# First projection of a hybrid decoder step: eight weight blocks loaded beside the first token tile, three token buffers, layer-norm rows in borrowed buffers

## Chip, cores and metric

One NeuronCore of a Trainium2 chip runs the whole program. The metric is device time in microseconds (us) of one execution; lower is better. The runs of the kernel before gave 1758.77 us (median of 3, from 1756.23 to 1762.34).

## What is computed

The reference is one layer of a decoder trunk on 1088 tokens (1024 of a prompt, 64 of eight samples). Only its first steps matter here:

```python
xp = layer_norm(x_prompt, ln_emb_g, ln_emb_b)        # 1024 tokens x 1024
xs = layer_norm(x_sample, ln_emb_g, ln_emb_b)        # 64 tokens x 1024
...
(a_b, a_c, a_h, g_q, g_k, g_v, g_gate, g_a, g_b, n_q, n_kv, n_win, n_gate) = split_in(x @ w_in)
...
def layer_norm(x, g, b):
    mu = jnp.mean(xf, axis=-1, keepdims=True)
    var = jnp.mean(jnp.square(xf - mu), axis=-1, keepdims=True)
    y = (xf - mu) * lax.rsqrt(var + LN_EPS) * g + b
```

Matmuls are made nearly exact by splitting both operands into a rounded high part and the rest, and adding three products (high x high, high x low, low x high).

## The kernel before

The program has four stages: phase_a (layer norm of the nine token tiles and the input projections, then the delta rule's preparation), attention woven with the delta rule and the samples' branch, the output projection, and the feed-forward stage. All loads and stores are issued by SP (SyncE), in one queue. The instructions of each engine are put in order by a scheduler when the program is built: it moves instructions past each other by its own estimate of when they can start, but on the chip each engine then follows its order strictly, and an instruction that waits holds up all behind it.

The change lies in the first part of phase_a (lines 271 to 354). It computes the 800 columns of w_in that belong to the keys, values, window rows and gates, by token tiles: nat = LN(x) @ w_in[:, those columns].

- **Weights.** Eight blocks of 128 rows x 792 columns (396 KB each, tile nraw, L302) are split into nh (rounded copy, ScalarE, L310) and nl (the rest, VectorE, L311; GpSimd for blocks 5 and 7, by SPP). Their raw buffers are four (NRAW). The eight remaining columns come as graw (two loads with runs of 16 bytes, L307).
- **Token tiles.** load_x(t) brings tile t (128 x 1024, 512 KB) into one of five buffers xt (L286). norm(t) (L290) normalises it in place, stores it to x0_d (L293; read again by a later stage) and transposes it with eight TensorE transposes into PSUM tiles tpx, from which ScalarE writes x0h (L173) and VectorE x0l (L175). The transposes share two PSUM buffers of tag tp with the setup transposes pcw and pst (L1835, L1850).
- **Layer norm** (L116 to L130): VectorE statistics (bn_stats, L121), GpSimd power for the inverse root (rs, L127), VectorE (x - mean) * gB (L128), ScalarE scaling by rs (L129), and the addition of bB, by VectorE for tiles 0 and 1 and by GpSimd from tile 2 on (LNV = 2, L130). gB and bB hold the two layer-norm rows on all 128 partitions; each comes as a 512 KB load that reads the same row 128 times (L297, L298).
- **Products.** rows(t) (L317) runs 48 matmuls pn of 400 columns for tile t (two halves of 24); tile 8 (the samples) has 32. The loop at L345 loads tile t+3, normalises tile t, and runs rows(t-1).

After it come the blocks of the delta rule (pjg), whose weights wra are loaded by load_w into the two buffers of pool wr (tag "wr") and split into wha and wla in pool wp (tags "wh" and "wl").

## Time and profile before

| | |
|---|---|
| median of the runs shown | 1758.77 us (1756.23 to 1762.34) |
| the profiled execution | 1755.33 us |
| its span, first to last instruction | 1753.6 us |
| PE (TensorE) busy | 1651.2 us, 94% |
| DVE (VectorE) | 901.8 us, 51% |
| ACT (ScalarE) | 654.8 us, 37% |
| POOL (GpSimd) | 607.0 us, 35% |
| granted TensorE clock, mean | 0.973 |

The span is read by stages. A stage in which PE is busy throughout is bound by its instructions; one with idle time is bound by what PE waits for there. The granted clock is given as a share of full speed: 1.00 is 2.4 GHz, 0.50 is 1.2 GHz.

### The profile page before, as it was taken

The page shows a single profiled execution, that of the slowest core. Times are in us where ns is not written, and L with a number is a line of the kernel's source. Part 1 is how long each engine was busy: PE and PEld are TensorE (multiplying, and loading weights), DVE is VectorE, ACT ScalarE, POOL GpSimd, SP SyncE. Part 2 cuts the span into 40 slices and gives each one's busy share as a digit, 9 for nine tenths or more (in the row PEclk, how much of TensorE's full clock was granted, in tenths as well). Part 3 has the DMA queues.
Part 4 walks back from the last instruction along what each step waited for, and adds up shares of the span by engine and source line. Part 5 has one row for each costly group of instructions (what it writes and reads, how often), then busy time and mean ns, then how long its engine had stood idle before and what let it go on. Part 6 is the DMA issues. An engine that isn't in the chain of part 4 may idle for free.

```text
span 1753.6 us, 26082 instructions
## 1 busy us (share of the span) xinstructions
PE 1651.2 (94%) x9683; PEld 1501.8 (86%) x9683; DVE 901.8 (51%) x2339; ACT 654.8 (37%) x1392; POOL 607.0 (35%) x514
## 2 busy tenths in 40 slices
PE   5999999998989999988799999999999999999995
PEld 4999999986867877776678999999999999999994
DVE  6444666466776678786765333332342323423237
ACT  4324552123575656565654312212222122221233
POOL 5322461222264323243544422323224132241326
PEclk9999999999698999999899999999999999999998
DMA  9622246536165454413132211112111111120102
GB/s 314 231 63 61 85 156 139 156 106 164 43 141 114 121 157 131 146 58 106 54 122 68 73 37 37 49 38 60 37 46 52 35 49 40 45 61 25 49 15 104
DMA packets 192492, 157.33 MB, mean 90 GB/s; under 512 B 60236, under 2 KB 165742, under 8 KB 192238
## 3 DMA queue, kind: packets, MB, share of 16 engines
q1 hardware_dynamic: 192366, 155.67, 30.1%
q8 instruction: 76, 1.25, 0.3%
q14 instruction: 50, 0.41, 0.1%
HBM read 116.72 MB, written 43.04 MB: 91 GB/s over the span
## 4 chain that ended last, share of the span: by engine, by line
PE 78%; DVE 8%; DMA 5%; ACT 3%; POOL 2%; issue 2%; SPq 2%; DVEq 0%; ACTq 0%; POOLq 0%
PE puv L207 5%; PE puv L205 5%; PE puv L206 5%; PE pug L205 5%; PE pug L206 5%; PE pug L207 5%; PE pd L206 4%; PE pd L205 4%; PE pd L207 4%; PE pas L1130 2%; PE pat L1189 2%; PE pao L1204 1%; PE pjg L207 1%; PE pjg L206 1%; PE pjg L205 1%
## 5 line engine op out<-in xcount | busy, mean ns | idle before, releaser
L197 POOL TENSOR_TENSOR wlf<-wrf,whf 128x1024 fp32r<-128x1024 f32 x44 | 105.5, 2398 | 318.7 <-ACT whf L196 296.3
L1792 DVE TENSOR_TENSOR acc<-acc,pd 128x512 f32<-128x512 f32 x146 | 99.4, 686 | 198.2 <-PE pd L207 162.4
L207 PE MATMUL puv<-x1l,whf 128*128 128x384 f32 (+1 forms) x528 | 173.1, 328 | 0.0
L205 PE MATMUL puv<-x1h,whf 128*128 128x384 f32 (+1 forms) x528 | 173.0, 328 | 0.0
L206 PE MATMUL puv<-x1h,wlf 128*128 128x384 f32 (+1 forms) x528 | 172.9, 328 | 0.0
L205 PE MATMUL pug<-x1h,whf 128*128 128x384 f32 (+1 forms) x528 | 172.8, 327 | 0.0
L206 PE MATMUL pug<-x1h,wlf 128*128 128x384 f32 (+1 forms) x528 | 172.4, 326 | 0.0
L207 PE MATMUL pug<-x1l,whf 128*128 128x384 f32 (+1 forms) x528 | 172.3, 326 | 0.0
L1748 ACT COPY fg<-pug 128x384 f32<-128x384 f32 (+1 forms) x88 | 31.9, 389 | 344.6 <-PE pug L207 344.6
L205 PE MATMUL pd<-dh,hs 128*128 128x512 f32 x352 | 138.1, 392 | 2.8 <-DVE acc L1790 2.5
L206 PE MATMUL pd<-dh,hs 128*128 128x512 f32 x352 | 138.0, 392 | 0.0
L207 PE MATMUL pd<-dl,hs 128*128 128x512 f32 x352 | 138.0, 392 | 0.0
L1165 POOL TENSOR_TENSOR ass<-ass,az 128x256 f32<-128x256 f32 (+6 forms) x56 | 71.7, 1299 | 165.6 <-DVE az L1159 91.3
L1769 POOL TENSOR_TENSOR dl<-wdr,dh 128x1024 fp32r<-128x1024 f32 x22 | 52.7, 2398 | 180.0 <-ACT dh L1768 180.0
L1130 PE MATMUL pas<-K,aq 128*128 128x320 f32 (+5 forms) x384 | 103.6, 372 | 8.8 <-DVE amx L1137 7.6
L233 DVE SCALAR_TENSOR_TENSOR fz<-fg,w_f,fz 128x1024 f32<-128x1024 f32 x88 | 88.8, 1061 | 28.3 <-ACT fz L231 28.3
L206 PEld LDWEIGHTS puv<-x1h,wlf 128*128 128x128 f32 x528 | 99.8, 189 | 2.1
L206 PEld LDWEIGHTS pug<-x1h,wlf 128*128 128x128 f32 x528 | 99.3, 188 | 2.0
L205 PEld LDWEIGHTS puv<-x1h,whf 128*128 128x128 f32 x528 | 99.8, 189 | 1.3
L207 PEld LDWEIGHTS pug<-x1l,whf 128*128 128x128 f32 x528 | 99.1, 188 | 1.8
L205 PEld LDWEIGHTS pug<-x1h,whf 128*128 128x128 f32 x528 | 99.2, 188 | 1.6 <-ACT x1h L173 0.2
L207 PEld LDWEIGHTS puv<-x1l,whf 128*128 128x128 f32 x528 | 99.7, 189 | 1.1
(586 smaller groups left out, 4277.2 us busy)
## 6 DMA issues: line engine op xcount, KB each, us to landing
wrf<-in_w_up_dram SPq DMA_DIRECT2D x44, 512.0 KB
wdr<-in_w_down_dram SPq DMA_DIRECT2D x22, 512.0 KB
aq<-q_d SPq DMA_DIRECT2D x32, 256.0 KB
wra<-in_w_in_dram SPq DMA_DIRECT2D x14, 512.0 KB
xt<-in_x_prompt_dram SPq DMA_DIRECT2D x8, 512.0 KB
x_d<-xt SPq DMA_DIRECT2D x8, 512.0 KB
sv_d<-gsv SPq DMA_DIRECT2D x8, 512.0 KB
ma_d<-gma SPq DMA_DIRECT2D x8, 512.0 KB
```

The costliest lines, as they stand in the source:

```text
L197: c.nc.gpsimd.tensor_tensor(lo, raw, hi, op=OP.subtract)
L205: c.nc.tensor.matmul(out, ah(k), bh(k), start=start and j == 0, stop=False)
L206: c.nc.tensor.matmul(out, al(k), bh(k), start=False, stop=False)
L207: c.nc.tensor.matmul(out, ah(k), bl(k), start=False, stop=stop and j == n - 1)
L233: nc.vector.scalar_tensor_tensor(o, src(i), wcol(i), o, op0=OP.mult, op1=OP.add)
L1130: nc.tensor.matmul(p[:, :step], u.q[:, h, 4 * kv + g0 + g], c.K[:, kk, ks], start=h == 0, stop=h == 1)
L1165: nc.gpsimd.tensor_tensor(x[:, g, :n], x[:, g, :n], z[:, b, g:g + 1].to_broadcast([128, n]), op=OP.mult)
L1189: nc.tensor.transpose(pt[:, a, g], (SW if b else SS)[:, g, t * 128:t * 128 + 128], c.ident)
L1204: nc.tensor.matmul(po, v, tl[:, a], start=False, stop=j + a == len(steps) - 1)
L1748: nc.scalar.copy(dst, b3(p[:, o:o + m]) if three else p[:, o:o + m])
L1769: nc.gpsimd.tensor_tensor(dl, raw, dh, op=OP.subtract)
L1792: nc.vector.tensor_tensor(a, a, p, op=OP.add)
```

## The change

1. The eight weight blocks are loaded in a row, right behind tile 0, before graw and the other token tiles. Six have a buffer each in their own pool; blocks 6 and 7 use one "wh" and one "wl" buffer of the delta rule's weights.
2. gB and bB live in the two "wr" buffers. Of each, SP loads one partition (4 KB); TensorE multiplies it by a row of ones (two matmuls of 512 columns each, plain f32), and ScalarE copies the products over gB and bB, on all partitions.
3. Token tiles have three buffers, not five, and the loop loads two ahead, not three.
4. All nl subtractions and all additions of bB are VectorE's.

```diff
-            wnr = e1.enter_context(tc.tile_pool(name="wr", bufs=NRAW, reuse_waits="tile"))
+            wnr = e1.enter_context(tc.tile_pool(name="wr", bufs=6, reuse_waits="tile"))
...
-            gB = wn.tile([128, D], F32, name="gB")
-            bB = wn.tile([128, D], F32, name="bB")
+            gB = wr.tile([128, D], F32, name="gB", tag="wr")
+            bB = wr.tile([128, D], F32, name="bB", tag="wr")
...
-                xts[t] = ld.tile([128, D], F32, name="xt", bufs=5)
+                xts[t] = ld.tile([128, D], F32, name="xt", bufs=3)
...
-                layer_norm(c, xts[t], r, gB, bB, xts[t], small, "0", nc.vector if t < LNV else nc.gpsimd)
+                layer_norm(c, xts[t], r, gB, bB, xts[t], small, "0", nc.vector)
...
             load_x(0)
-            nc.sync.dma_start(gB, bcast(I["ln_emb_g"], D))
-            nc.sync.dma_start(bB, bcast(I["ln_emb_b"], D))
+            for x, y in ((gB, "ln_emb_g"), (bB, "ln_emb_b")):
+                nc.sync.dma_start(x[0:1], bcast(I[y], D, 1))
             raws8 = []
             for k in range(KD):
-                raw = wnr.tile([128, 792], F32, name="nraw")
-                held = nc.sync.dma_start(raw, w_in[k * 128:(k + 1) * 128, 2312:3104])
+                pool, tag = ((wnr, "nraw"), (wp, "wh"), (wp, "wl"))[max(k - 5, 0)]
+                raw = pool.tile([128, 792 if k < 6 else 1024], F32, name="nraw", tag=tag)[:, 0:792]
+                nc.sync.dma_start(raw, w_in[k * 128:(k + 1) * 128, 2312:3104])
                 raws8.append(raw)
-                if k == 1:
-                    graw = wn.tile([128, KD, 8], F32, name="graw")
-                    for j, s in enumerate((1796, 1792)):
-                        nc.sync.dma_start(graw[:, :, 4 * j:4 * j + 4], w_in[:, s:s + 4].rearrange("(k p) n -> p k n", p=128))
-                if k == 0:
-                    norm(0)
-                nc.scalar.copy(nh[:, k, 0:792], raw)
-                (nc.gpsimd if k in SPP else nc.vector).tensor_tensor(nl[:, k, 0:792], raw, nh[:, k, 0:792], op=OP.subtract)
+            graw = wn.tile([128, KD, 8], F32, name="graw")
+            for j, s in enumerate((1796, 1792)):
+                nc.sync.dma_start(graw[:, :, 4 * j:4 * j + 4], w_in[:, s:s + 4].rearrange("(k p) n -> p k n", p=128))
+            load_x(1)
+            one = wn.tile([1, 128], F32, name="one")
+            nc.vector.memset(one, 1.0)
+            for x in (gB, bB):
+                for h in range(2):
+                    p = c.ps.tile([128, 512], F32, name="pgB", tag="mm", bufs=c.nb["mm"])
+                    nc.tensor.matmul(p, one, x[0:1, 512 * h:512 * h + 512], start=True, stop=True)
+                    nc.scalar.copy(x[:, 512 * h:512 * h + 512], p)
+            norm(0)
+            for k in range(KD):
+                nc.scalar.copy(nh[:, k, 0:792], raws8[k])
+                nc.vector.tensor_tensor(nl[:, k, 0:792], raws8[k], nh[:, k, 0:792], op=OP.subtract)
...
-            load_x(1)
-            load_x(2)
...
-                if t + 3 < NT:
-                    load_x(t + 3)
+                if t + 2 < NT:
+                    load_x(t + 2)
```

What the scheduler makes of it, at three places. A row is an instruction: line, operation, output <- inputs, shape; x3 stands for three in a row. In the changed file the lines of the layer norm and of transpose_split are 2 smaller, those of setup 4 larger.

**VectorE, from the first statistics on.** xt_112 is token tile 0, xt_135 tile 1, xt_199 tile 2 of the changed program; nraw are the weight blocks in their order. Before:

```order
L121 BN_STATS st0_118<-xt_112 128x6 x2
L123 BN_AGGR mv0_121<-st0_118 128x2
L125 TENSOR_SCALAR ve0_123<-mv0_121 128x1
L128 SCALAR_TENSOR_TENSOR xt_112<-xt_112,mv0_121,gB_107 128x1024
L130 TENSOR_TENSOR xt_112<-xt_112,bB_108 128x1024
L311 TENSOR_TENSOR nl_110<-nraw_116,nh_109 128x792
L311 TENSOR_TENSOR nl_110<-nraw_147,nh_109 128x792
L313 TENSOR_TENSOR nl_110<-graw_149,nh_109 128x8x8
L175 TENSOR_TENSOR x0l_86<-tpx0_131,x0h_85 128x4x128
```

And with the change, behind the same three rows:

```order
L317 TENSOR_TENSOR nl_110<-nraw_120,nh_109 128x792
L126 SCALAR_TENSOR_TENSOR xt_112<-xt_112,mv0_154,gB_107 128x1024
L317 TENSOR_TENSOR nl_110<-nraw_122,nh_109 128x792
L317 TENSOR_TENSOR nl_110<-nraw_124,nh_109 128x792
L317 TENSOR_TENSOR nl_110<-nraw_126,nh_109 128x792
L128 TENSOR_TENSOR xt_112<-xt_112,bB_108 128x1024
L317 TENSOR_TENSOR nl_110<-nraw_128,nh_109 128x792
L317 TENSOR_TENSOR nl_110<-nraw_130,nh_109 128x792
L319 TENSOR_TENSOR nl_110<-graw_132,nh_109 128x8x8
L119 BN_STATS st0_203<-xt_135 128x6 x2
L173 TENSOR_TENSOR x0l_86<-tpx0_164,x0h_85 128x4x128
L119 BN_STATS st0_288<-xt_199 128x6 x2
```

All eight blocks now stand ahead of tile 0's x0l (two blocks stand ahead of the first row shown), and the statistics of tile 1 do too; before, only two blocks and graw did.

**SP's queue after tile 2's load (changed program).** out_5 are the eight copies of the samples' old window rows from DRAM to DRAM, cw and strow the setup loads, xt_201, xt_286 and xt_371 tiles 3, 4 and 5.

```order
L286 DMA xt_199<-in_x_prompt_dram 128x1024
L1835 DMA cw_381<-in_conv_a_w_dram 6x128
...
L1744 DMA out_5_dram<-in_cache_nsa_win_dram 16x8064 x3
L291 DMA x0_d_63<-xt_112 128x1024
L1744 DMA out_5_dram<-in_cache_nsa_win_dram 16x8064 x5
L286 DMA xt_201<-in_x_prompt_dram 128x1024
L291 DMA x0_d_63<-xt_135 128x1024
L291 DMA x0_d_63<-xt_199 128x1024
L337 DMA kw_d_66<-nat_230 128x768
L339 DMA out_2_dram<-nat_230 128x512
L286 DMA xt_286<-in_x_prompt_dram 128x1024
L286 DMA xt_371<-in_x_prompt_dram 128x1024
```

Before, tiles 1 to 4 were loaded ahead of the out_5 copies, and only tile 5 stood behind seven of them. Now tiles 3 and on stand behind all eight.

**TensorE, from the end of tile 2's products to the beginning of tile 3's (changed program).** pn_496 is the second half of tile 2, tpx0_455 and tpx0_462 are tile 3's transposes, tpx0_540 the first of tile 4's, pn_555 and pn_581 tile 3's two halves.

```order
L205 MATMUL pn_496<-nl_110,x0h_85 128x400
L1854 MATMUL pst_420<-ident_74,strow_418 128x88
L1854 MATMUL pst_426<-ident_74,strow_424 128x88
L1854 MATMUL pst_432<-ident_74,strow_430 128x88
L1854 MATMUL pst_438<-ident_74,strow_436 128x88
L169 MATMUL tpx0_455<-ident_74,xt_201 128x128 x4
L169 MATMUL tpx0_462<-ident_74,xt_201 128x128 x4
L203 MATMUL pn_555<-nh_109,x0h_85 128x400
L203 MATMUL pn_581<-nh_109,x0h_85 128x400
L169 MATMUL tpx0_540<-ident_74,xt_286 128x128 x4
```

On VectorE the copies out of those pst tiles stand behind tile 5's layer norm (the rows between the last two copies are memsets of later masks and are not shown):

```order
L126 SCALAR_TENSOR_TENSOR xt_371<-xt_371,mv0_615,gB_107 128x1024
L1856 COPY st_g_377<-pst_404 128x3x6 x7
L1856 COPY st_g_377<-pst_415 128x3x6
L128 TENSOR_TENSOR xt_286<-xt_286,bB_108 128x1024
L128 TENSOR_TENSOR xt_371<-xt_371,bB_108 128x1024
L1856 COPY st_f_378<-pst_420 128x2x22 x2
L1856 COPY st_f_378<-pst_426 128x2x22 x2
L336 COPY gab_105<-nat_469 128x32
L1856 COPY st_f_378<-pst_432 128x2x22 x2
L1856 COPY st_f_378<-pst_438 128x2x22 x2
...
L173 TENSOR_TENSOR x0l_86<-tpx0_455,x0h_85 128x4x128
```

Before, the setup transposes were spread over the middle of tiles 1 and 2, with 24 matmuls between one pair and the next; now four of them stand in a row at the boundary of tiles 2 and 3. From the tile products on, TensorE's order is the same in both programs until the attention stage has begun, differs there (about 1,500 rows in which neighbours change places), and is the same again from the output projection's end on.

## Rows read from the trace of the kernel before

**Rows 1.** The page: the span, each engine's busy time, and the chain that ended last, by engine.
```profile
span 1753.6 us, 26082 instructions
...
PE 1651.2 (94%) x9683; PEld 1501.8 (86%) x9683; DVE 901.8 (51%) x2339; ACT 654.8 (37%) x1392; POOL 607.0 (35%) x514
...
PE 78%; DVE 8%; DMA 5%; ACT 3%; POOL 2%; issue 2%; SPq 2%; DVEq 0%; ACTq 0%; POOLq 0%
```
**Rows 2.** Busy time by stage: stretch (us), its length, busy us of PE, PEld (weight loads), DVE, ACT, POOL with instructions, granted clock, DMA share, GB/s.
```profile
0.00:40.30 40.30, 20.16 (x96) 17.61 (x96) 28.07 (x57) 18.89 (x24) 18.59 (x17) 0.92 0.94 312
40.30:109.66 69.36, 69.36 (x400) 68.40 (x401) 25.06 (x58) 18.25 (x33) 21.67 (x14) 1.00 0.50 188
109.66:400.00 290.34, 283.93 (x1759) 268.69 (x1759) 172.10 (x448) 107.83 (x216) 98.57 (x119) 1.00 0.40 111
400.00:910.00 510.00, 455.21 (x2940) 380.25 (x2939) 366.52 (x1237) 289.90 (x768) 195.28 (x184) 0.93 0.41 113
910.00:1753.60 843.60, 822.51 (x4494) 766.88 (x4492) 310.08 (x542) 219.96 (x353) 272.88 (x181) 0.99 0.16 50
```
**Rows 3.** The chain of waits at the first part: start, us, what. One row for the eight transposes ahead of the products of tiles 4 to 7.
```profile
65.48 0.87 PE tpx L171 x8
...
75.12 0.87 PE tpx L171 x8
...
84.74 0.87 PE tpx L171 x8
...
94.37 0.64 PE tpx L171 x8
```
**Rows 4.** TensorE in order of time: start, us, instruction, [idle before <- releaser]: its start, its wait in tile 0, two matmuls of tile 8 that follow each other, and the first of the delta rule's blocks.
```profile
11.08 1.94 PE L171 MATMUL tpx<-ident,xt 128*128 128x128 f32 x8 [11.08 <-DVE xt L130]
...
23.94 0.70 PE L205 MATMUL pn<-nh,x0h 128*128 128x400 f32 x1 [5.78 <-ACT nh L310]
...
108.93 0.35 PE L214 MATMUL pn<-nh,x 128*128 128x400 f32 x1
109.11 0.35 PE L215 MATMUL pn<-nl,x 128*128 128x400 f32 x1
...
109.66 0.34 PE L205 MATMUL pjg<-x0h,wha 128*128 128x384 f32 x1
```
**Rows 5.** SP's issues of weight blocks 4 to 7, with start and us.
```profile
18.60 0.36 SPq L302 DMA_DIRECT2D nraw<-in_w_in_dram  x1
...
20.48 0.33 SPq L302 DMA_DIRECT2D nraw<-in_w_in_dram  x1
...
22.12 0.35 SPq L302 DMA_DIRECT2D nraw<-in_w_in_dram  x1
...
23.52 0.52 SPq L302 DMA_DIRECT2D nraw<-in_w_in_dram  x1
```
**Rows 6.** The first 60 us, by tile: operation, count, shortest/median/longest ns, first and last start, shapes: first the instructions on xt, then those on nraw, then x0l.
```profile
L121 DVE BATCH_NORM_STATS2 st<-xt x12: 643/680/695, 4.4 to 44.1; 128x6 f32<-128x512 f32 x12
L128 DVE SCALAR_TENSOR_TENSOR xt<-xt,mv,gB x6: 1277/1281/2833, 7.1 to 47.0; 128x1024 f32<-128x1024 f32 x6
L129 ACT ACTIVATE xt<-xt,rs x6: 1147/1150/1152, 8.5 to 48.7; 128x1024 f32<-128x1024 f32 x6
L130 DVE TENSOR_TENSOR xt<-xt,bB x2: 1175/1200/1225, 9.7 to 23.9; 128x1024 f32<-128x1024 f32 x2
...
L310 ACT CAST nh<-nraw x8: 834/852/860, 9.6 to 31.6; 128x792 fp32r<-128x792 f32 x8
L311 DVE TENSOR_TENSOR nl<-nraw,nh x6: 973/978/985, 10.9 to 30.0; 128x792 fp32r<-128x792 f32 x6
...
L175 DVE TENSOR_TENSOR x0l<-tpx,x0h x9: 677/692/692, 12.8 to 56.9; 128x512 fp32r<-128x512 f32 x9
```
**Rows 7.** VectorE's first wait for a load, and ScalarE's copy of a product out of PSUM (the nearest row to the copies of gB and bB).
```profile
4.42 1.28 DVE L121 BATCH_NORM_STATS2 st<-xt 128x6 f32<-128x512 f32 x2 [2.84 <-DMA xt<-in_x_prompt_dram]
...
45.99 0.49 ACT L326 COPY nat<-pn 128x400 f32<-128x400 f32 x1 [3.92 <-PE pn L207]
```
**Rows 8.** The columns of rows 2, over the first loads: gB and bB until about 6, then weight blocks, graw from about 9, weight blocks and token tiles from 11.
```profile
3.50:6.00 2.50, 0.00 (x0) 0.00 (x0) 1.51 (x4) 0.00 (x0) 0.00 (x0) 1.00 1.02 261
6.00:8.50 2.50, 0.00 (x0) 0.00 (x0) 1.42 (x2) 0.00 (x0) 0.55 (x1) 1.00 1.01 400
8.50:11.00 2.50, 0.00 (x0) 0.00 (x0) 1.29 (x2) 2.39 (x3) 0.00 (x0) 1.00 0.85 140
14.00:18.00 4.00, 4.00 (x22) 3.82 (x21) 4.00 (x6) 1.16 (x2) 0.00 (x0) 1.00 0.97 376
```
**Rows 9.** TensorE, two plain f32 matmuls of 512 columns that follow each other, and what such a group's instructions take each.
```profile
207.79 1.02 PE L661 MATMUL pgg<-gZ,gkT 128*128 128x512 f32 x2
...
L661 PE MATMUL pgg<-gZ,gkT x32: 590/592/595, 206.8 to 276.2; 128*128 128x512 f32 x32
```
**Rows 10.** The columns of rows 2, around the first idle time of TensorE: the granted clock is the third figure from the end.
```profile
0.00:11.00 11.00, 0.00 (x0) 0.00 (x0) 4.86 (x10) 3.89 (x5) 1.24 (x7) 1.00 0.80 223
11.00:18.00 7.00, 6.92 (x32) 6.33 (x32) 6.57 (x10) 3.18 (x6) 0.00 (x0) 1.00 0.98 361
18.00:21.00 3.00, 0.16 (x1) 0.00 (x0) 3.00 (x8) 0.00 (x0) 0.73 (x1) 1.00 1.01 359
21.50:24.00 2.50, 0.06 (x1) 0.06 (x1) 2.50 (x7) 2.00 (x2) 1.51 (x2) 0.50 0.87 273
24.00:27.50 3.50, 3.35 (x12) 2.79 (x12) 3.50 (x7) 2.45 (x3) 1.82 (x2) 0.50 0.94 273
28.00:28.50 0.50, 0.16 (x1) 0.16 (x2) 0.50 (x1) 0.29 (x1) 0.50 (x1) 1.00 1.10 374
```
**Rows 11.** SP's issue of the out_5 copies and of tile 5 behind them, and VectorE's wait for that tile.
```profile
25.47 5.63 SPq L1740 DMA_DIRECT2D out_dram<-in_cache_nsa_win_dram  x7
31.59 0.35 SPq L288 DMA_DIRECT2D xt<-in_x_prompt_dram  x1
...
43.49 1.29 DVE L121 BATCH_NORM_STATS2 st<-xt 128x6 f32<-128x512 f32 x2 [0.85 <-DMA xt<-in_x_prompt_dram]
```
**Rows 12.** A pair of setup transposes and the copies out of one of them.
```profile
45.79 0.32 PE L1850 MATMUL pst<-ident,strow 88*128 88x88 f32 x2
...
46.07 0.54 DVE L1852 COPY st_f<-pst 128x44 f32<-128x44 f32 x4 [1.29 <-PE pst L1850]
```

More of the change, by code (lines that the diff above doesn't have):

```diff
@@ L46 @@
 NRAW = 4
-LNV = 2
 ENDS = 2
@@ L50 @@
 GSV = 3
-SPP = (5,7)
 ORDER = (0, 1, 2, 3, 4, 5, 6, 7)
```

## The prediction

> **What bounds the kernel now.** First the page: PE is busy for 1651.2 of 1753.6 us, and the chain that ended last lies on PE for 78% [rows 1]. So only PE's idle time can be won, and the next view is busy time by stage [rows 2]: PE lacks 20.1 us in the first 40.3 us, nothing from there to 109.66, 54.8 us in the attention stretch (400 to 910), and little elsewhere. The change works on the first stretch.
>
> How much is lost there is worked out from its end. From 40.3 to 109.66 PE is never idle [rows 2], and a tile recurs every 9.63 us [rows 3]: 0.87 for eight transposes and 48 matmuls at 0.182, the distance of two that follow each other [rows 4], 8.76. Eight tiles are 77.0 us, tile 8 is 32 x 0.182 + 0.64 = 6.5, the eight setup transposes about 1.2 (pairs of 0.32 [rows 12]): 84.7 us. The delta rule's first block begins at 109.66 [rows 4], so the stage runs as if PE had begun at **25.0** and never waited. Where the 25 us go: PE first works at 11.08, then waits in tile 0 for nh of weight block 4 until 23.94 [rows 4]. Blocks 4 to 7 are issued only from 18.6 on, when the four raw buffers come free [rows 5]. Meanwhile the clock has fallen to half and comes back at about 28 [rows 10].
>
> **The change, part by part. Loads.** Tile 0 is seen at 4.42 [rows 7]. Before, gB and bB (1 MB) followed; now two single rows do, so the weight blocks move ahead of 1 MB. Eight blocks of 0.406 MB at the 400 GB/s of the stretch from 6 to 8.5 [rows 8] are 1.01 us each. At that rate tile 0's bytes are through near 3.75, and I keep a lag of 0.7 to 1.0 from last byte to use, as tile 0 shows. Blocks are seen at 5.6, 6.6 and so on to 12.7. graw's short runs cost about 2.5 us at 140 GB/s [rows 8] wherever they stand; behind the blocks they end near 14.4, and tiles 1 and 2 (0.52 MB each at 376 GB/s [rows 8]) are seen at about 17 and 18.
>
> The Trainium skill, "DMA: Bandwidth & Descriptors", section Specifications, gives some 358 GB/s as what HBM yields to one core. The stretch at 400 GB/s speaks against taking it here; by it the blocks would come every 1.13 us, tile 1 at nearly 18, and the gain below would be about 2.1 instead of 2.5.
>
> **The rows of the layer norm.** Four f32 matmuls of 512 columns, each two passes at a distance of 1.02 - 0.59 = 0.43 us [rows 9]: 3.5 us, in which PE has nothing else to do. Four copies out of PSUM at some 0.5 (0.49 for 400 columns [rows 7]) stand between ScalarE's weight copies. ScalarE's stream from 5.6 on is 8 x 0.85 + 4 x 0.5 + 1.15 [rows 6], about 10 us: its last nh ends near 15.5. The single-row load has no row; I take 0.5 us behind tile 0, and up to 2 us more is covered, since the copy of gB's second half stands behind three weight copies (until 8.7).
>
> **Tile 0.** VectorE's order now decides. By its durations [rows 6] and ScalarE's stream: blocks 0 to 2 until 9.8, (x - mean) * gB until 11.1, blocks 3 to 5 until 14.3 (block 5 waits for nh, which waits for the scaling of tile 0), + bB until 15.5, blocks 6 and 7 until 17.4, graw, then the statistics of tile 1 (1.3) and x0l of tile 0 (0.7): **19.6**. PE's transposes can run from 15.5, two high matmuls at 17, the rest from 19.6. Before, PE began at 11.08 but stood still later; now all weights are there.
>
> **The clock.** PE is idle from about 8 to 15.5. Before, the level fell about 3 us after PE had gone idle at 18.2, and came back about 4 us after it resumed at 23.94 [rows 10]. The same here puts the transposes and at most 4 us of matmuls at half speed, 0 to 2 us; I take 1.0. The level is 1.00 from the start although PE is idle [rows 10].
>
> **Tiles 1 to 3.** Tiles 1 and 2 are normalised by 26 and 27, ahead of their use at 29 (19.6 + 46 x 0.182 + 1.0). Tile 1's products end at 39.5, tile 2's at 48.9 (with four setup transposes). Then the chain of setup transposes costs: two, their copies on VectorE (0.54 [rows 12]), two more, their copies, tile 3's transposes (which need the same two PSUM buffers), its x0l, and the first transposes of tile 4, ahead of which x0l must have freed a buffer. VectorE's copies stand behind the layer norms of tiles 4 and 5. Their loads wait for stores and for three buffers to come free, and I put them at about 40.6 and 42, counting the bytes ahead in SP's queue at 0.37 MB per us. Step by step, tile 3's third matmul starts near 54.5 instead of 51.2. Between 1.5 (VectorE free) and 5 (tile 5 two us later) I take a loss of **3.0**.
>
> **Sum for the stage.** 19.6 less 1.24 for work done before it (eight transposes, two matmuls) + 1.0 + 3.0 = 22.4 against 25.0: the stage ends **2.5 us** sooner (rounded), near 107.2.
>
> **At nothing:** the bB additions on VectorE (1.2 each) and blocks 5 and 7 (1.0 each) lie beside 9.63 us of PE per tile, of which VectorE then uses some 6; the delta rule's first weights, which now wait until the last layer norm frees gB and bB near 70, have until 107 (load, copy and subtraction need under 8). Three token buffers suffice from tile 6 on, since loads come two tiles, 19 us, ahead. If that cover is gone, PE waits at a tile's transposes.
>
> **Behind the stage.** PE's order is the same up to the beginning of attention, so the gain is passed on. In the attention stretch neighbours change places; nothing says in which direction that goes. It has 54.8 us of idle PE and a mean clock of 0.93, another 36 us [rows 2]; I take 0, and as bounds a tenth of the 91, 9 us either way.
>
> The profiled execution took 1755.33, 3.4 less than the median shown; less 2.5 it is 1752.8. Against the median of 1758.77 I forecast **1756.3**.
>
> **The rivals.**
> *No stall at tile 3 and no lost clock.* If VectorE reaches tile 5 sooner (its loads are light by then) and the clock is back at 19.6, 1.0 + about 2.5 of the 3.0 come back: 6.0 gained, 1752.8. For: 54.5 hangs on two load times which I estimated. Against: four setup transposes and tile 3's stand behind each other on two buffers whatever the loads do.
>
> *Tile 3 comes late.* Now all eight out_5 copies (4.1 MB) stand ahead of tile 3, and VectorE's statistics of tile 3 stand ahead of x0l of tile 2's second half. Before, tile 5 behind seven of them was used 11.9 us after its issue (31.59 to 43.49 [rows 11]). I expect tile 3 at about 34, issued near 25 once tile 0's store is through. It decides from 38 on: PE needs that x0l at 41.8, and the statistics, two short steps, the multiplication and x0l take 3.7. At 43.5 PE would lose 5.5: net 3.0 slower, 1761.8. Against: 1 MB of gB and bB and two tiles less are ahead of it than were ahead of tile 5.
>
> *The attention stretch gets worse.* Each engine follows its new order strictly; where a new neighbour waits longer, all behind it waits. A tenth of that stretch's loss is 9 us: 1758.8 - 2.5 + 9.0 = **1765.3**, slower than before. It decides once it costs more than the 2.5 gained. The same in the other direction gives 1747.3. For either: some 1,500 rows of PE's order there have new neighbours, and those of VectorE and ScalarE too; against: the same work, the same dependences.
>
> **How the numbers follow.** About 0.3%, 5.3 us, is what a measurement of this kernel tells from no change: faster means under 1753.5, slower over 1764.1. Chances: the forecast 0.47; no stall 0.20; tile 3 late 0.12; attention worse 0.13; attention better 0.08. Faster: 0.12 of the second, the 0.08, and 0.05 from the forecast's own spread (clock and stall at their low ends): 0.25. Slower: 0.10 of the attention case and 0.03 of the late tile: 0.13. The same: 0.62. The range goes from 1748, between the two fast cases, to 1764, short of the worst one.
>
> **What would show it.** Right: gB and bB by four matmuls before 9; block 7 split by 17.5; PE's steady work on tile 0 from 19 to 20; tile 1 and 2 without waits; PE idle for some 3 us at tile 3 with VectorE's setup copies as releaser; pjg from 107. Wrong: VectorE waiting for a load of tile 1 or tile 3 with PE idle behind it; the copies of gB late, so that + bB ends after 16; pjg before 104.5 or after 109.7. If pjg comes at 107 and the time still differs by more than 5 us, the attention stretch did it.

## The result, and the profile after

The changed kernel takes 1766.22 us (median of 20 runs, 1759.35 to 1772.41), the kernel before in the same comparison 1758.34 (20 runs): ratio **1.0051**, 95% interval 1.0039 to 1.0063. It is 7.9 us slower, 0.45%, more than the 0.3% that the prediction took as the least difference that can be told. The forecast was 1756.3, in a range from 1748 to 1764.

| | before | after |
|---|---|---|
| profiled execution, its span | 1755.33, 1753.6 | 1769.43, 1767.7 |
| a second profiled execution, its span | 1759.95, 1758.3 | 1763.02, 1761.3 |
| first pjg (end of the first stage) | 109.7, 110.1 | 114.7, 115.1 |
| first pas to first pwo (attention) | 391.4, 392.9 | 393.9, 394.9 |

The names are PSUM tiles: pjg of the delta rule's first blocks, pas of the attention scores, pwo of the output projection. The two executions of one kernel differ by 5 to 6 us, those of different kernels that were recorded first by 14. Two boundaries repeat within a few tenths to 1.5 us: the end of the first stage, 5.0 later than before, and the length of attention, 2 to 2.5 longer. These are what the experiments go by.

The stages of the changed kernel, columns as in [rows 2]; the stretches end at the first pjg, the first pas and the first pwo:

```profile
0.00:40.30 40.30, 30.53 (x122) 24.64 (x123) 23.29 (x38) 17.46 (x26) 4.03 (x9) 1.00 0.85 285
40.30:60.00 19.70, 15.42 (x77) 13.29 (x77) 17.97 (x69) 6.27 (x9) 7.01 (x14) 0.90 0.63 232
60.00:114.70 54.70, 54.70 (x309) 54.19 (x308) 20.55 (x34) 15.63 (x26) 12.57 (x16) 0.97 0.47 156
...
446.90:840.80 393.90, 359.05 (x2366) 301.29 (x2366) 291.19 (x1030) 229.13 (x647) 147.59 (x148) 0.93 0.42 113
```

PE is idle for 9.8 us in the first stretch instead of 20.1, as the change intends. But from 40.3 to 60, where [rows 2] had no idle time, 4.3 are lost, with VectorE busy for 18.0 of 19.7, and the clock falls. TensorE in order of time, columns as in [rows 4]: the broadcast, tile 0, and its waits up to tile 3:

```profile
4.58 3.75 PE L312 MATMUL pgB<-gB,one 1*128 1x512 f32 x4 [4.58 <-DMA gB<-in_ln_emb_g_dram]
8.13 3.62 PE L312 MATMUL pgB<-bB,one 1*128 1x512 f32 x4
16.05 1.94 PE L169 MATMUL tpx<-ident,xt 128*128 128x128 f32 x8 [4.31 <-DVE xt L128]
...
19.67 0.70 PE L204 MATMUL pn<-nh,x0l 128*128 128x400 f32 x1 [0.82 <-DVE x0l L173]
20.17 0.54 PE L205 MATMUL pn<-nl,x0h 128*128 128x400 f32 x1
20.50 0.54 PE L203 MATMUL pn<-nh,x0h 128*128 128x400 f32 x1
...
43.72 0.25 PE L1854 MATMUL pst<-ident,strow 32*128 32x32 f32 x1 [1.33 <-DVE x0l L173]
...
52.80 0.39 PE L1854 MATMUL pst<-ident,strow 88*128 88x88 f32 x2
55.37 0.48 PE L1854 MATMUL pst<-ident,strow 88*128 88x88 f32 x2 [2.17 <-DVE st_f L1856]
56.13 1.91 PE L169 MATMUL tpx<-ident,xt 128*128 128x128 f32 x8 [0.28 <-DVE st_f L1856]
...
59.39 1.12 PE L169 MATMUL tpx<-ident,xt 128*128 128x128 f32 x4 [0.49 <-DVE x0l L173]
60.16 0.68 PE L204 MATMUL pn<-nh,x0l 128*128 128x400 f32 x1
...
114.71 0.34 PE L203 MATMUL pjg<-x0h,wha 128*128 128x384 f32 x1
```

Tile 0's products begin at 19.67 but follow each other at 0.33 (20.17, 20.50), not at the 0.182 of [rows 4]. PE waits for VectorE's x0l, and at the boundary of tiles 2 and 3 for its copies out of pst. Why VectorE is late there: SP's issues, SP's longest waits from 20 to 62 us (line, releaser: total, times, longest), and VectorE:

```profile
21.75 0.52 SPq L291 DMA_DIRECT2D x_d<-xt  x1
22.31 3.35 SPq L1744 DMA_DIRECT2D out_dram<-in_cache_nsa_win_dram  x5
30.05 0.36 SPq L286 DMA_DIRECT2D xt<-in_x_prompt_dram  x1
...
41.45 1.56 SPq L286 DMA_DIRECT2D xt<-in_x_prompt_dram  x2
```
```profile
SPq L286 <- DMA x_d<-xt: 13.2, 3, 8.1
```
```profile
40.15 1.29 DVE L119 BATCH_NORM_STATS2 st<-xt 128x6 f32<-128x512 f32 x2 [5.90 <-DMA xt<-in_x_prompt_dram]
...
52.69 2.35 DVE L128 TENSOR_TENSOR xt<-xt,bB 128x1024 f32<-128x1024 f32 x2
54.96 0.52 DVE L1856 COPY st_f<-pst 128x44 f32<-128x44 f32 x4
...
56.18 0.30 DVE L480 MEMSET mG<- 128x128 f32 x2
...
58.67 0.67 DVE L173 TENSOR_TENSOR x0l<-tpx,x0h 128x512 fp32r<-128x512 f32 x1
```

With three buffers a load waits until the tile three before it is stored, and the stores stand among the 4.1 MB of out_5 copies: tile 3 is issued at 30.05 (8.3 after tile 0's store), tile 4 at 41.45. VectorE then has the layer norms of tiles 3, 4 and 5 in a row, and the copies that PE waits for stand behind them. Behind those copies stand 2.5 us of memsets for later masks (from 56.18), and only then tile 3's x0l. The clock (third figure from the end) around both places:

```profile
22.00:24.00 2.00, 2.00 (x8) 1.98 (x7) 2.00 (x3) 0.66 (x1) 2.00 (x2) 1.00 0.84 258
24.00:26.00 2.00, 2.00 (x9) 1.99 (x8) 1.60 (x3) 1.65 (x2) 0.56 (x1) 1.00 0.72 194
26.00:28.00 2.00, 2.00 (x13) 2.00 (x12) 1.00 (x1) 0.00 (x0) 0.00 (x0) 1.00 0.58 222
...
56.00:58.00 2.00, 1.86 (x9) 1.67 (x9) 1.80 (x14) 0.59 (x1) 0.65 (x3) 0.55 1.02 391
58.00:60.00 2.00, 1.51 (x6) 0.98 (x6) 1.77 (x9) 0.58 (x1) 1.94 (x9) 0.50 0.71 226
60.00:62.00 2.00, 2.00 (x9) 1.99 (x8) 0.69 (x1) 0.58 (x1) 1.80 (x7) 0.50 0.71 248
62.00:64.00 2.00, 2.00 (x10) 1.99 (x9) 1.60 (x5) 0.00 (x0) 0.18 (x1) 0.75 0.00 0
```

After the 3 us of idle time the level is 0.50 (1.2 of 2.4 GHz) until about 63. At 22 to 26 it is given as 1.00, but only 8 or 9 matmuls fit into 2 us, as at 60 to 62 at half level; from 26 on there are 13.

### The profile page after: what moved, and what is told of

It is laid out like the page before. It is cut to its first block, busy times and chain, and to the rows that moved or that the text cites. A ratio compares the mean times of both kernels' runs of the same rounds, so it can differ in the third digit from the quotient of the medians.

```text
span 1767.7 us, 26091 instructions
## 1 busy us (share of the span) xinstructions
PE 1673.3 (95%) x9691; PEld 1518.8 (86%) x9691; DVE 909.2 (51%) x2349; ACT 651.9 (37%) x1394; POOL 585.1 (33%) x505
## 4 chain that ended last, share of the span: by engine, by line
PE 57%; DVE 5%; ACT 3%; DMA 3%; issue 2%; POOL 2%; SPq 1%; DVEq 0%; ACTq 0%; POOLq 0%
PE puv L205 5%; PE puv L204 5%; PE puv L203 5%; PE pug L203 5%; PE pug L204 5%; PE pug L205 5%; PE pd L204 4%; PE pd L203 4%; PE pd L205 4%; PE pas L1134 2%; PE pat L1193 2%; PE pao L1208 2%; PE pao L1207 1%; DMA svw<-in_cache_nsa_win_dram 1%; DVE atl L1204 1%
## 5 line engine op out<-in xcount | busy, mean ns | idle before, releaser
L1204 DVE TENSOR_TENSOR atl<-pat,ath 128x512 fp32r<-128x512 f32 (+1 forms) x136 | 89.7, 668 | 25.5 <-ACT ath L1202 24.7
```

Source lines behind the costliest of these rows:

```text
L1204: nc.vector.tensor_tensor(tl[:, :k], pt[:, :k], th[:, :k], op=OP.subtract)
```

## The experiments

Three theories of what makes the loss: **1**, three buffers and loads behind the out_5 copies; **2**, setup transposes in a row at tiles 2 and 3, and the fallen clock behind them; **3** (from the third set on), the order which the scheduler gives the attention stretch. Edits of the changed kernel, used alone and together:

```diff
x5:     xt bufs=3 -> 5, load_x(t + 2) -> load_x(t + 3), load_x(2) ahead of the loop
aux:    pcw, pst: tag="tp" -> tag="aux"        (po: -> tag="po"; mix: pcw "po", pst "aux")
pool:   layer_norm(..., nc.vector) -> nc.vector if t < 2 else nc.gpsimd
late n: the out_5 copies ordered behind the x0_d store of tile n
bcast:  dma_start(x[0:1], bcast(I[y], D, 1)) -> dma_start(x, bcast(I[y], D)); pgB removed
warm n: n x matmul(pwarm, c.ident, raws8[2][:, 512 columns]) ahead of norm(0)
```

**Both kernels again.**

> The kernel before, unchanged, profiled a second time, to tell what differs between two executions of one program. If the stage boundaries are a property of the program: pjg begins at 109.7 +- 0.3, pks at 409 +- 2, pas at 435 +- 2, pug at 941 +- 2, span 1753.6 +- 3. If the later stages vary from one execution to the next by their clock alone, pjg stays at 109.7 but pks, pug and the end move by up to 8 us, and the mean granted clock moves with them (0.965 to 0.976).

> The changed kernel, unchanged, profiled a second time. By the theory that the loss is made in the first stage (tile 3 late, setup transposes in a row, then the fallen clock) pjg begins at 114.6 +- 0.5 again and PE's idle time between 40 and 60 us is again 4.3. By the rival that half of the loss is made later and by chance of the execution, pjg is the same, but the 11.5 us by which pks stood behind the kernel before come out at 5 to 14.

The first pjg is at 110.1 and 115.1: the 5.0 is a property of the programs. From pjg to the end the first pair of executions differs by 9.1 (1643.9, 1653.0), the second by -2.0 (1648.2, 1646.2): of the 9.1 us that lie behind the first stage in the first pair, most is chance.

**a_x5** (edit x5).

> The changed kernel with five token buffers and loads three tiles ahead, as before; all else of the change is kept. Theory 1 (three buffers and loads behind the eight out_5 copies are the cause): tile 3's statistics on VectorE begin by 34 instead of 40.15, the 1.33 of waiting at the setup transposes (43.7) goes, the boundary of tiles 2 and 3 shrinks from 3.0 of idle PE to under 1, the level stays at 1.00 at 56 to 63, pjg begins near 107 to 109, and the time falls by 6 to 8 us to about 1758 to 1760 (ratio to the kernel before 1.000). Theory 2 (four setup transposes in a row on two PSUM buffers, behind VectorE's norms, are the cause, whatever the loads do): the 1.33 goes, but 2 to 3 us of idle PE and the fallen clock at the boundary stay, pjg 112 to 113.5, ratio 1.003 to 1.005.

Both missed: pjg 116.3, ratio 1.0090 (1.0064 to 1.0115). The loads came early, and VectorE's layer norms took the place ahead of x0l of tile 1. TensorE, as above:

```profile
31.34 0.63 PE L203 MATMUL pn<-nh,x0h 128*128 128x400 f32 x2 [0.24 <-ACT x0h L171]
33.70 1.11 PE L169 MATMUL tpx<-ident,xt 128*128 128x128 f32 x4 [1.73 <-DVE x0l L173]
```

Four norms in a row fill VectorE from 23 to 33; PE waits and the clock falls, here at tile 1 and again at the transposes. At the boundary of tiles 2 and 3 PE still waits 3.2. Late loads alone are not the cause.

**a_setup6** (`SETUP = 3` -> `SETUP = 6`).

> The changed kernel with the setup (its loads, transposes and copies) placed in the program after tile 5 instead of tile 2 (SETUP 6); three token buffers and late loads are kept. Theory 2 (setup transposes in a row at tiles 2 and 3, then the fallen clock): no idle PE at the boundary of tiles 2 and 3, level 1.00 from 26 us on, pjg at 108 to 109 (114.6 less 3.0 idle less 3.2 of clock), ratio 0.999 to 1.001. Theory 1 (late tiles): PE waits instead at tile 3's own transposes or at those of tile 4 or 5, with a load as VectorE's releaser; pjg 111 to 114, ratio 1.003 to 1.005.

The boundary of tiles 2 and 3 is clean (0.4 idle, level 1.00), but the transposes now cost 2.4 idle and a level of 0.50 at 80 to 90: pjg 113.6, where theory 2 had expected 108 to 109. The stall follows the transposes. The loads are as late here as before, so at tile 3 a late tile costs only these 0.4. The time, 1.0076 (1.0046 to 1.0107), is worse all the same: most of it is lost behind the first stage.

**a_aux**, **a_aux_x5**, **a_nocopy** (the out_5 copies left out), **a_poolb** (edit pool).

> The changed kernel, but the setup transposes (pcw, pst) write to the two PSUM buffers of tag aux, which nothing else uses at this time, instead of the two that the token transposes use. The order on TensorE then has no more than two of them in a row, none between tile 2's products and tile 3's transposes. Theory 2 (the transposes in a row on shared buffers, with the fallen clock behind them): idle PE from 40 to 60 us falls from 4.3 to about 1.3 (the wait for tile 3's load stays, now at tile 3's or tile 2's transposes), the level stays 1.00, pjg at 108 to 109.5 instead of 114.9, and the time about 6 us under the changed kernel's 1766: ratio to the kernel before 0.999 to 1.002. Theory 1 (late loads and three buffers): PE waits for tile 3, 4 or 5 instead, pjg 111 to 114. If the first stage's 5 us are not passed on to the end, pjg comes early and the ratio stays at 1.005.

> The same with five token buffers and loads three tiles ahead, so that tiles 3 and 4 are loaded ahead of the out_5 copies. If late tiles cost what the other PSUM buffers leave (1.3 us), pjg is 1 to 1.5 earlier than in the run with the other buffers alone. If, as five buffers alone showed, the early tiles only let VectorE's layer norms crowd in ahead of x0l of tile 1 (1.73 idle and a fallen level at 33), that loss of 1.7 + 1.4 stays and pjg is 1 to 2 later than with the other buffers alone.

> The changed kernel without the eight out_5 copies (4.1 MB of the samples' old window rows are not written); three token buffers stay. Theory 1 (the loads behind the copies): tile 3 is used by 32 to 35 instead of 40.15, the 1.33 of waiting at 43.7 goes and VectorE is through with tiles 4 and 5 when the setup transposes come, so the 3.0 at 52 to 60 falls under 1 and the level holds: pjg 107 to 109. Theory 2: the four transposes in a row still wait for VectorE's copies on two buffers, 2 to 3 us idle with a fallen level: pjg 111.5 to 113.5.

> The changed kernel with the additions of bB from tile 2 on back on GpSimd; TensorE's and SP's order in the first stage stay. If VectorE's two additions of tiles 4 and 5 (52.7 to 55.0), which stand ahead of the copies out of pst, make the stall at the boundary of tiles 2 and 3, its 3.0 fall to about 1 and the level holds: pjg 110 to 111. If the stall comes from the chain on two buffers alone, it stays at 2.5 to 3 and pjg at 114 to 115; GpSimd's addition takes longer than VectorE's 1.2, so tile 3 may come up to 1.3 later, which PE then waits for at 43.7.

a_aux ends the stage at 109.3 at a level of 1.00, as theory 2 said, although its tile 3 is as late (used at 39.6); 3.3 of waiting for late tiles is left. a_aux_x5 is later (113.5: the crowd on VectorE). a_nocopy is at 114.9: tile 3 is used at 26.2, and theory 1 fails again (1.9 idle at tile 1, 2.2 at the boundary). a_poolb is at 114.6. From 40 to 75 us, columns as above, a_aux and then a_nocopy:

```profile
40.00:60.00 20.00, 18.14 (x108) 17.75 (x107) 16.70 (x50) 6.55 (x10) 10.75 (x21) 1.00 0.65 235
60.00:75.00 15.00, 13.53 (x79) 12.79 (x78) 12.41 (x19) 5.10 (x8) 2.55 (x2) 1.00 0.57 202
```
```profile
40.00:60.00 20.00, 17.78 (x100) 16.09 (x99) 11.80 (x58) 5.82 (x9) 3.63 (x9) 0.99 0.42 151
60.00:75.00 15.00, 15.00 (x82) 14.90 (x83) 11.03 (x18) 5.38 (x8) 5.31 (x12) 0.91 0.46 158
```

In a_nocopy and a_poolb 1.33 and 1.22 of the wait at the boundary are for tile 3's x0l, behind the memsets; in a_nocopy VectorE had even stood idle for 3.4 ahead of the copies. So the transposes in a row cost whether or not the tiles are late, and of the single reliefs so far only separate PSUM buffers help by more than 1.5. But a_aux took 1.0110 (1.0092 to 1.0129), a_aux_x5 1.0121 and a_poolb 1.0111, a_nocopy 1.0018: attention had become 411, 414, 408 and 389 us long. That gave theory 3.

**aux_x5_pool**, **aux_l5_pool**, **aux_l5_pool_w** (late 5; four extra matmuls from blocks 2 and 3), **a_bcast**.

> The changed kernel with setup transposes on the aux buffers, five token buffers (loads three ahead) and the additions of bB from tile 2 on back on GpSimd. Its order on TensorE from the first pjq to the first pug is, row for row, that of the kernel before. Theory 3 (the order which the scheduler gives the attention stretch sets its length: 391 to 393 from the first pas to the first pwo in the kernel before, 394 to 395 in the changed one, 401 to 414 in four of the variants so far): 389 to 394 here, where the two runs with the other PSUM buffers had 411 and 414, and pjg to the end takes 1644 to 1650. If the length of that stretch hangs on something else that these edits share (buffers, tiles kept longer), it stays over 400. First stage: with four tiles loaded early VectorE's norms crowd ahead of x0l of tile 1, as with five buffers alone (1.4 to 2.0 idle, fallen level); pjg 111 to 113.5; time 1757 to 1763, ratio 0.999 to 1.003.

> The changed kernel with setup transposes on the aux buffers, the additions of bB from tile 2 on back on GpSimd, and the eight out_5 copies held behind tile 5's store in SP's order (an ordering edge, no wait); three token buffers stay. If the losses of the first stage are the three named (late tile 3, transposes in a row, VectorE's crowd), idle PE from 24 to 75 us is under 1.5 and the level 1.00 there, and what is left is the start: pjg at 105.5 to 107.5, earlier than the kernel before's 109.9. If three token buffers cost by themselves, PE waits at tiles 4 to 6 and pjg is 108 to 110. Its order in the attention stretch has not been run before; by theory 3 that stretch takes 390 to 414, whatever the first stage does.

> The same with four extra f32 matmuls (identity by weight blocks 2 and 3, 512 columns each, results unused) between the broadcast of bB and tile 0's transposes, where TensorE otherwise is idle from 11.7 to 16. If the half-speed spacing of tile 0's first 9 to 17 products comes from that idle time, they come at 0.18 apart from the first one on and pjg is 1.4 to 2.6 earlier than without the extra matmuls. If TensorE runs at half speed there because of something else (waits for operands, the start of the program), the spacing stays 0.33 and pjg is the same or up to 1 later.

> The changed kernel with gB and bB loaded as before (two loads of 512 KB that read a row 128 times) instead of one partition each and four matmuls. The weight blocks come 2.5 later (1 MB at 400 GB/s), tile 0 is normalised near 11 instead of 16, and ScalarE is spared 2. By the prediction's own sum the broadcast by TensorE gains about 2.5 for the weights but makes tile 0's rows 4 to 5 later: which of them decides shows in the start of tile 0's products. If the rows decide, they run from 14 to 16 on, block by block, and pjg is 1 to 4 earlier than the changed kernel's 114.9; if the weights decide, they end later than in the changed kernel and pjg is 115 to 118. Attention by its own order: the same on TensorE as the run with other buffers and five token tiles, so by theory 3 its 414 from pas to pwo.

aux_x5_pool bears theory 3 out: pjg 111.2, attention 393.8, ratio 1.0004 (0.9989 to 1.0019). aux_l5_pool misses: pjg 112.2, with 3.2 idle at tile 1, attention 408.2, ratio 1.0083. With the extra matmuls pjg is 108.4, with 1.9 idle, attention 395.7, ratio 1.0019; their last pair takes 1.02, as in [rows 9], and tile 0's products follow at 0.18 from the start:

```profile
16.79 1.02 PE L319 MATMUL pwarm<-nraw,ident 128*128 128x512 f32 x2
17.64 1.04 PE L169 MATMUL tpx<-ident,xt 128*128 128x128 f32 x8
...
22.30 0.34 PE L205 MATMUL pn<-nl,x0h 128*128 128x400 f32 x1
22.48 0.34 PE L203 MATMUL pn<-nh,x0h 128*128 128x400 f32 x1
```

So the half speed there comes from TensorE's idle time before. a_bcast is faster than both kernels: 1749.16, ratio 0.9952 (0.9936 to 0.9969). Its tile 0 runs from 14.2, so the rows of the layer norm had decided, not the weights: making them on TensorE cost more than the earlier weights gave. pjg is 111.7, with 4.6 idle at the transposes. The rest of its gain is attention, 383.9. The 414 expected for that rested on an error: row by row its order on TensorE is not a_aux_x5's.

**bc_po_pool**, **bc_mix_pool**, **bc_po_l3_pool**, **bc_po_x5_pool** (bcast and pool in all; po, mix, po with late 3, po with x5).

> The changed kernel with three edits: gB and bB by two 512 KB loads as before (no broadcast on TensorE), setup transposes in the PSUM buffer of tag po, additions of bB from tile 2 on back on GpSimd. Eight weight blocks at once, three token buffers and nl on VectorE stay. First stage: a_bcast's 111.7 less its 4.6 of idle time at the setup transposes and 3 to 4 of fallen level behind it: pjg at 103 to 105.5 (if theory 2 is wrong and tile 3's load behind the out_5 copies decides, PE waits at tile 3 instead and pjg stays at 108 or later). Attention: its order from pkc to pug is that of a_bcast on TensorE, VectorE, ScalarE and SP; theory 3 says 382 to 387 from the first pas to the first pwo. Time: a_bcast's 1749 less 6 to 8: 1741 to 1743, ratio 0.990 to 0.993. If attention goes by chance, 384 to 414 and a time of 1742 to 1772.

> As bc_po_pool, but pcw in tag po and the pst transposes in the two buffers of tag aux, so that they come earlier and in pairs. VectorE copies eight st_a and eight st_g pieces ahead of x0l of tile 1: PE may wait there for up to 2 with the level falling once; pjg 103.5 to 107. The same order in attention as a_bcast and bc_po_pool: 382 to 387 by theory 3; time 1741 to 1746.

> As bc_po_pool, with the out_5 copies held behind tile 3's store in SP's order. Its order in attention is that of the kernel before on TensorE, VectorE, ScalarE and SP: by theory 3 390 to 394 from pas to pwo, and from pjg to the end the kernel before's 1644 to 1648. First stage as bc_po_pool, or earlier by what tile 3's load costs there: pjg 102.5 to 105.5. Time: 5 to 7 under the kernel before, 1751 to 1753, ratio 0.996 to 0.997. This is what the first stage alone is worth.

> As bc_po_pool, with five token buffers and loads three ahead. Its order in attention is that of a_aux on TensorE, VectorE, ScalarE and SP: by theory 3 408 to 413 from pas to pwo, so that in spite of a first stage that ends 3 to 6 sooner than the kernel before's (pjg 104 to 107, with some crowding of VectorE ahead of x0l of tile 1) the time is 1767 to 1772, ratio 1.006 to 1.009. If the first stage is what counts and attention goes by chance, 1750 to 1760.

pjg 112.2 (a miss: 2.4 idle at tile 1 for the addition of bB, 2.9 at a setup transpose ahead of tile 4), 105.8, 104.9 and 110.7; attention 382.2, 387.7, 392.7 and 417.1, each within a few us of its order's value; ratios 0.9975 (0.9958 to 0.9993), **0.9939** (0.9921 to 0.9956), 0.9965 (0.9948 to 0.9982) and 1.0081 (1.0052 to 1.0110). bc_mix_pool, 1747.35, is the fastest. The first stages of bc_mix_pool and bc_po_l3_pool came as expected, that of bc_po_x5_pool 4 later; of the four times only bc_po_l3_pool's (1751.98) lies in its expected range.

**a_warm3**, **a_warm2** (edit warm; nothing of the change is undone).

> The changed kernel with three extra f32 matmuls (identity by weight block 2, 512 columns, results unused) between the broadcast of bB and tile 0's transposes, where TensorE is otherwise idle from 11.7 to 16. Nothing of the change is undone. From pkc to pug its order on all five engines is that of a_bcast. Theory 3: 382 to 388 from the first pas to the first pwo (the changed kernel has 394 to 395). Clock: tile 0's products come at 0.18 from the first one or two on instead of at 0.33 until 25, and pjg is 1.5 to 2.6 earlier, 112.3 to 113.5; if the spacing has another cause, pjg stays at 114.5 to 115.5. Time by both: the changed kernel's 1766 less 2 for the clock, less 8 to 12 for the order: 1752 to 1756, ratio 0.997 to 0.999. If the order is not what decides, 1763 to 1766.

> The same with two extra matmuls. From pkc to pug its order on all five engines is that of the changed kernel, so by theory 3 393 to 396 from pas to pwo, and the time is the changed kernel's less what the first stage gives. The extra work ends near 15, leaving about 1.5 idle ahead of tile 0's transposes: if that is short enough for the level to hold, pjg is 1.5 to 2.6 earlier and the time 1764, ratio 1.003 to 1.004; if not, nothing changes, pjg 114.7 to 115.1 and ratio 1.004 to 1.006.

a_warm3: tile 0's products at 0.18 from the first on, yet pjg is 114.7 (a miss):

```profile
20.12 0.45 PE L204 MATMUL pn<-nh,x0l 128*128 128x400 f32 x1 [1.75 <-DVE x0l L173]
20.41 0.34 PE L205 MATMUL pn<-nl,x0h 128*128 128x400 f32 x1
...
55.12 0.49 PE L1858 MATMUL pst<-ident,strow 88*128 88x88 f32 x2 [2.18 <-DVE st_f L1860]
```

PE comes to the boundary 2 us sooner and waits there until 55.12, as it did until 55.37: VectorE's chain at the boundary sets the end of the stage. Attention is 388.3 and the ratio 0.9998 (0.9978 to 1.0017), a time of 1757.69. a_warm2 keeps the changed kernel's order: attention 394.7, pjg 115.0, ratio 1.0032 (1.0011 to 1.0053), 1766.20 in the same comparison. One more unused matmul is worth 8.5 us with the first stage ending 0.3 apart; what differs behind it is the order.

The runs that share an order of instructions from pkc (just ahead of attention) to pug (the feed-forward stage) on TensorE, VectorE, ScalarE and SP, compared row by row (the other four kernels have orders of their own, with pas to pwo of 395.7 to 414.1; the last column is the difference of the medians to the kernel before in the same comparison, less that of pjg to 109.9, the mean of its two executions):

| order of | runs | pas to pwo | left |
|---|---|---|---|
| a_bcast | a_bcast, bc_po_pool, bc_mix_pool, a_warm3 | 383.9, 382.2, 387.7, 388.3 | -10.5, -7.7, -7.1, -7.1 |
| before | before (two), aux_x5_pool, bc_po_l3_pool, a_nocopy | 391.4, 392.9, 393.8, 392.7, 388.6 | 0, -0.1, -1.5, -2.0 |
| after | after (two), a_warm2 | 393.9, 394.9, 394.7 | +2.9, +1.1 |
| a_setup6 | a_setup6, a_poolb | 407.0, 407.8 | +13.1, +16.6 |
| a_aux | a_aux, bc_po_x5_pool | 411.0, 417.1 | +18.5, +15.6 |

What differs inside, in the stretch from pas to pwo of the kernel before, a_aux and a_bcast (columns as above), and what pas (the attention scores) waited for on TensorE there:

```profile
435.40:826.80 391.40, 357.31 (x2365) 299.37 (x2364) 286.79 (x1028) 230.81 (x646) 147.96 (x147) 0.93 0.41 112
```
```profile
PE pas L1130 <- DVE amx L1137: 6.2, 12, 1.1
```
```profile
436.30:847.30 411.00, 365.73 (x2365) 307.62 (x2365) 297.65 (x1032) 233.39 (x650) 148.90 (x149) 0.91 0.41 111
```
```profile
PE pas L1134 <- DVE amx L1141: 11.8, 19, 2.0
```
```profile
440.90:824.80 383.90, 352.16 (x2366) 297.49 (x2366) 290.36 (x1030) 229.38 (x646) 147.58 (x147) 0.94 0.43 116
```
```profile
PE pas L1127 <- DVE amx L1134: 3.8, 8, 0.8
```

The same 2365 or 2366 matmuls; idle 34, 45 and 32 us, the wait for VectorE's maxima (amx) 6.2, 11.8 and 3.8, and the busy time grows with the fallen clock. That the order makes the difference is inferred from runs that share one; which neighbours make the waits was not traced further.

## Why the prediction was wrong

The forecast was a first stage 2.5 us shorter, passed on to the end. It came out 5.0 longer, and 1 to 3 came on top. The sum of the prediction had PE as if it began at 22.4; here is each term against what was measured.

- **The start was right.** + bB ends at 15.9 (predicted 15.5), x0l of tile 0 at 19.6 (19.6), tiles 1 and 2 wait for no load. Only pgB took 7.2 instead of 3.5, at half speed, without a consequence of its own.
- **The step that failed: the price of the boundary of tiles 2 and 3.** The sum had 3.0 of waiting there and put the clock behind it at nothing. The mechanism was right: setup transposes and tile 3's on two PSUM buffers, with VectorE's copies behind the norms of tiles 4 and 5. So was the idle time, 2.9 (2.17 + 0.28 + 0.49). But the level is 0.50 from 56 to 63, which adds 3 to 3.5, and tile 3's third matmul starts at 60.16, not 54.5. That this place decides the stage is shown by a_aux: with PSUM buffers of their own for the setup transposes, which also spreads them, and a tile 3 as late, the level stays at 1.00 and the stage ends at 109.3, 5.4 sooner; and in a_setup6 wait and fallen clock go where the transposes go. The memsets ahead of tile 3's x0l, which the sum does not name, are part of it.
- **Tile 3's load was mis-timed, but does not make the loss alone.** I put it at 34, "issued near 25 once tile 0's store is through", and gave the rival with a late tile 3, which decides from 38 on, a chance of 0.12. It was issued at 30.05 and used at 40.15. The store had stood among the out_5 copies. The Trainium skill, "DMA: Bandwidth & Descriptors", section "Queues, rings and completion order", says that each DMA engine consumes its ring's descriptors in order; tile 0's store, issued at 21.75 behind three copies, with tile 3's issue held until 30.05, agrees. In a_nocopy, without the copies, the store was issued at 20.09 and the load at 22.77. The late tile cost the 1.33 of waiting at 43.72 and moved the norms of tiles 4 and 5 into the boundary. But with early tiles the stage ends no sooner (a_nocopy 114.9, a_x5 116.3): the norms then stand ahead of x0l of tile 1.
- **The clock at the start was mis-sized.** "The level is 1.00 from the start although PE is idle" [rows 10] is what the record says, not what TensorE does: products at 0.33 until 25.2 cost 2.6 where I took 1.0. The Trainium skill, "TensorE: Matmul & The Clock Gate", section "What's actually happening", says that the throttled state is the default and that activity releases it; the spacing agrees, and so do the extra matmuls.
- **The sum, term by term.** The stage behaves as if PE had begun at 114.7 - 84.7 = 30.0, 7.6 over the 22.4: 1.6 from the clock at the start, 1.3 from the late tile, some 3.4 from the second fall, and about 1.3 in gaps too small to place. The shares are not independent: a_warm3 took the first away, and the boundary ate it.
- **The additions "at nothing"** hold as far as the end of the stage goes: back on GpSimd (a_poolb) it is 114.6. But VectorE is not at "some 6" of 9.63 us where it matters: from 40.3 to 60 it is busy for 18.0 of 19.7.
- **"Three token buffers suffice from tile 6 on"** holds (PE is never idle from 60 to 114.7), but five do not mend tiles 3 to 5: with them VectorE's norms crowd in earlier.
- **Behind the stage** the offset was passed on, plus the order's own difference: the bounds of "9 us either way" were wide enough here, but the orders found span 29 us in the last column of the table above, far more than the 1.7 to 3 between these two kernels.

In all 5.0 from the first stage, 1 to 3 from the order; the rest of the 7.9 is within its interval (6.9 to 11.1).

## What to carry to other kernels

Price a wait of TensorE with the clock behind it: here 2.9 us of idle time brought 7 us at half level. Count what is queued on an engine ahead of the next thing that TensorE waits for: norms, additions, setup copies and memsets shared VectorE here, and earlier tiles or fewer additions moved the wait but not the end of the stage; PSUM buffers of their own for the setup transposes did. A buffer that comes free only with a store is late by what stands around that store in the DMA queue: 8.3 us from store to load with the out_5 copies, 2.7 without. Where a scheduler orders a long later stage by its own estimates, judge an early edit by its stage's boundary, and compare the orders behind it before believing the total: here a third unused matmul was worth 8.5 us.

## What the runs showed of the hardware

The granted clock is shown as 1.00 before its first recorded change although matmuls come at half speed: in the changed kernel 0.33 instead of 0.182 for 400 columns until 25.2, in the kernel before 1.94 for tile 0's eight transposes [rows 4] instead of 0.87 [rows 3]. And VectorE is stretched by GpSimd's additions: in aux_l5_pool, VectorE's rows and GpSimd's rows at the same time,

```profile
28.11 2.62 DVE L128 TENSOR_TENSOR xt<-xt,bB 128x1024 f32<-128x1024 f32 x1
...
34.22 2.06 DVE L338 COPY gab<-nat 128x32 f32<-128x32 f32 x1 [0.47 <-ACT nat L332]
```
```profile
27.24 2.40 POOL L128 TENSOR_TENSOR xt<-xt,bB 128x1024 f32<-128x1024 f32 x1 [1.26 <-ACT xt L127]
...
33.89 2.35 POOL L128 TENSOR_TENSOR xt<-xt,bB 128x1024 f32<-128x1024 f32 x1 [1.26 <-ACT xt L127]
```

The addition takes 2.62 instead of 1.22 and ends 1.1 after GpSimd's; the copy of 32 columns takes 2.06 instead of 0.17 in the changed kernel and ends with GpSimd's. So moving bB back to GpSimd is not free for VectorE.
